# Strided slice: loads into 64 partitions with two rows each, one batch per queue, and joined stores

## Chip, cores, metric

One core of one Trainium2 chip. The metric is device time in microseconds (us) of one launch; a lower number is better. Each experiment was timed beside the kernel before on the same chip. A ratio is the mean time of one kernel's fast runs over that of the other's fast runs of the same rounds, so it is not quite the ratio of the medians that are quoted; a run that counts as slow is in the median and range, but not in the ratio. Faster or slower needs 2%; ratios are quoted with their 95% intervals.

## The reference

```python
# x is float32 [32, 1024, 512]; start, stop, stride = 0, 512, 2
def reference(x, start, stop, stride):
    return x[:, start:stop:stride, :].astype(np.float32)
```

The output is [32, 256, 512]: 256 rows of 2 KB out of each of 32 batches, every second row of the first half. 16.8 MB are read and 16.8 MB are written. Nothing is computed.

## The kernel before

Each batch has its 256 rows split by parity. Half of them go straight from HBM (the main memory) to HBM, issued by POOL. The other half go into SBUF (the memory on the core, 128 partitions), loaded by the queues of SP and ACT, and out again by SP's queue. SP, ACT and POOL are the units of the core that issue the transfers; one set of 16 DMA engines carries out those of all three queues (their shares of its time add up to 95.1%). `apart` chooses the parity, which alternates from one pair of batches to the next.

```python
def apart(b):
    return 1 - (b >> 1 & 1)

def two(t, b, step, parity):
    return t[b : b + step + 1 : step].rearrange("b (p two) d -> two p b d", two=2)[parity]

def tile_strided_slice_kernel(tc, x, start, stop, stride, out):
    ...                                                   # src = x[:, 0:512:2, :], P = 128, D = 512
        held = [io.tile([P, 2, D], x.dtype, name=f"held{i}") for i in range(B // 2)]
        for g in range(0, B, EIGHT):
            for i, (b, step) in enumerate(((0, 5), (2, 5), (1, 3), (3, 3))):
                b += g
                at = g + 2 * i
                (sp, act)[i % 2].dma_start(held[at // 2], two(src, at, 1, 1 - apart(at)))
                pool.dma_start(two(out, b, step, apart(b)), two(src, b, step, apart(b)))
        for b in range(B):
            to = out[b].rearrange("(p two) d -> two p d", two=2)[1 - apart(b)]
            sp.dma_start(to, held[b // 2][:, b % 2])
```

A load fills 128 partitions with one row of each of two batches (512 KB, "128x2" below). A store writes one batch (256 KB). There are 16 loads, 16 copies and 32 stores.

## Time and profile before

| | before |
|---|---|
| median (range), us | 80.34 (80.07 to 80.65), 4 runs |
| profiled execution, us; its span | 79.17; 77.4 |
| DMA queues | q1 = SP (loads, then stores), q10 = ACT (loads), q0 = POOL (copies) |
| first packet of SP, ACT, POOL, us | 1.83, 2.53, 6.21 |
| last packet of ACT's loads, of POOL's copies, us | 49.1, 55.7 |

The last packets are read from the packet records of the trace. The profiled execution of before is a little faster than its timed runs, so the two profiles lie 3.6 us apart where the medians lie 2.6 apart. The prediction's 80.57 us is the median of three runs.

### The profile page before, as it was taken

How to read it: one execution, taken by the hardware profiler on the slowest of the kernel's cores; microseconds unless marked ns; L12 is line 12 of the kernel's file. 1: busy time of each engine (PE TensorE's matmuls, PEld its weight loads, DVE VectorE, ACT ScalarE, POOL GpSimd, SP SyncE). 2: the span in 40 equal slices, each digit the busy share in tenths (PEclk: the TensorE clock that was granted, in tenths of full speed). 3: DMA queues.
4: the chain of work that ended last, by engine and by line, in shares of the span. 5: the costliest groups of instructions: out<-in, count | busy, mean ns of one | idle time of the engine just before them, and what ended most of it. 6: DMA issues, size and time to landing. Idle time of an engine off the chain costs nothing. (4 is left out here: it accounts for less than half of the span.)

```text
span 77.4 us, 113 instructions
## 1 busy us (share of the span) xinstructions
POOL 11.3 (15%) x20
## 2 busy tenths in 40 slices
POOL 4995003303023031130000000000000000000000
DMA  0799999999999999999999999999999999999960
GB/s 7 235 303 334 332 281 347 327 310 386 351 349 363 364 314 358 358 321 333 323 300 310 347 307 357 413 392 339 402 404 405 375 356 347 361 356 353 350 216 20
DMA packets 11264, 25.17 MB, mean 325 GB/s; under 512 B 1024, under 2 KB 1024, under 8 KB 11264
## 3 DMA queue, kind: packets, MB, share of 16 engines
q1 hardware_dynamic: 6784, 12.59, 48.1%
q0 software_dynamic: 2304, 8.39, 29.3%
q10 hardware_dynamic: 2176, 4.19, 17.7%
HBM read 16.78 MB, written 16.78 MB: 434 GB/s over the span
## 5 line engine op out<-in xcount | busy, mean ns | idle before, releaser
L37 POOL DMA_DIRECT2D out_dram<-in_x_dram x16 | 11.1, 696 | 22.6 <-DMA out_dram<-in_x_dram 21.8
L57 POOL MEMSET const-float32-0.0<- 128x1 f32 x1 | 0.1, 99 | 0.2 <-issue 0.2
L57 POOL MEMSET const-bfloat16-1.0<- 128x1 bf16 x1 | 0.1, 102 | 0.0
L57 POOL MEMSET const-uint8-127<- 128x1 uint8 x1 | 0.1, 100 | 0.0
L57 POOL MEMSET const-float32-1.0<- 128x1 f32 x1 | 0.1, 99 | 0.0
## 6 DMA issues: line engine op xcount, KB each, us to landing
out_dram<-in_x_dram POOLq DMA_DIRECT2D x16, 512.0 KB, 23.6
out_dram<-held SPq DMA_DIRECT2D x32, 256.0 KB, 6.1
held<-in_x_dram ACTq DMA_DIRECT2D x8, 512.0 KB, 22.9
held<-in_x_dram SPq DMA_DIRECT2D x8, 512.0 KB, 22.7
```

Of the source, the lines that this page charges most:

```text
L37: pool.dma_start(two(out, b, step, apart(b)), two(src, b, step, apart(b)))
L57: nc = _bacc.Bacc("TRN2", target_bir_lowering=False, num_devices=1)
```

## The change

The intent: one store of 512 KB for two neighbouring batches, half as many stores and waits. For this a partition must hold two rows of one batch, so the even batch of a pair goes to partitions 0 to 63 by SP's queue, the odd one to 64 to 127 by ACT's. Loads are now 32 of 256 KB ("64x2" below). The order of issue is fixed as written.

```diff
+def pairs(t, parity):
+    return t.rearrange("(p n two) d -> two p n d", n=2, two=2)[parity]
 ...
-    with tc.tile_pool(name="io", bufs=1) as io:
+    with tc.tile_pool(name="io", bufs=1) as io, tc.manual_schedule():
 ...
-                at = g + 2 * i
-                (sp, act)[i % 2].dma_start(held[at // 2], two(src, at, 1, 1 - apart(at)))
+                for k, queue in enumerate((sp, act)):
+                    at = g + 2 * i + k
+                    to = held[at // 2][P // 2 * k : P // 2 * (k + 1)]
+                    queue.dma_start(to, pairs(src[at], 1 - apart(at)))
                 pool.dma_start(two(out, b, step, apart(b)), two(src, b, step, apart(b)))
-        for b in range(B):
-            to = out[b].rearrange("(p two) d -> two p d", two=2)[1 - apart(b)]
-            sp.dma_start(to, held[b // 2][:, b % 2])
+        for b in range(0, B, 2):
+            to = out[b : b + 2].rearrange("b r d -> (b r) d")
+            sp.dma_start(pairs(to, 1 - apart(b)), held[b // 2])
```

## The prediction

> **What bounds the kernel now.** I read the page's busy slices first, then its queues, then the windows, then SyncE's waits. The kernel computes nothing: half of the rows go from HBM to HBM by POOL's queue, the other half into SBUF by the queues of SP and ACT, and out again by SP's. The slices and the queues of the page:
>
> ```profile
> DMA  0799999999999999999999999999999999999960
> GB/s 7 235 303 334 332 281 347 327 310 386 351 349 363 364 314 358 358 321 333 323 300 310 347 307 357 413 392 339 402 404 405 375 356 347 361 356 353 350 216 20
> DMA packets 11264, 25.17 MB, mean 325 GB/s; under 512 B 1024, under 2 KB 1024, under 8 KB 11264
> q1 hardware_dynamic: 6784, 12.59, 48.1%
> q0 software_dynamic: 2304, 8.39, 29.3%
> q10 hardware_dynamic: 2176, 4.19, 17.7%
> ```
>
> The 16 DMA engines are busy (9) from the third slice to the third from last, and the three queues' shares add to 95.1%. So the time is the packets' time: it can only fall if a packet gets cheaper, or fewer bytes move. 25.17 MB is 8.39 MB each of direct copies, loads and stores. Take 16 completion packets per transfer off: ACT's q10 has 8 transfers, so 2176 - 128 = 2048 packets for 4.19 MB, 2 KB each; POOL's q0 has 16, so 2304 - 256 = 2048 packets for 8.39 MB, 4 KB each. A mean packet took 0.177 x 16 x 77.4 us / 2048 = 107 ns on q10, and likewise 97 ns on SP's q1 (6144 packets of 2 KB), 177 ns on q0.
>
> The windows over the stages (us, POOL busy, clock, DMA share, GB/s):
>
> ```profile
> 1.80:6.20 4.40, 4.40 (x8) 1.00 0.87 270
> 6.20:49.00 42.80, 6.16 (x9) 1.00 1.00 336
> 49.00:56.00 7.00, 0.00 (x0) 1.00 1.02 383
> 56.00:60.00 4.00, 0.00 (x0) 1.00 1.06 407
> 60.00:72.00 12.00, 0.00 (x0) 1.00 1.06 357
> 72.00:77.40 5.40, 0.00 (x0) 1.00 0.53 184
> ```
>
> With loads in flight, engines that are just as busy move 336 GB/s; when only stores are left they reach 407, then 357. At 407 a 2 KB packet costs 16 x 2048 / 407 = 80 ns, so the 97 to 107 ns above hold a good deal of waiting inside packets. Measured against 407, the stretch 6.2 to 49 loses 42.8 x (1 - 336/407) = 7.5 us, 60 to 72 loses 1.5, and the end 72 to 77.4 loses 5.4 - 0.99/0.407 = 3.0, mostly engines that finish at different times, and the closing. That is all there is to win.
>
> SyncE's waits (total us, times, longest) and the issues:
>
> ```profile
> SPq L40 <- DMA held<-in_x_dram: 22.0, 4, 6.5
> SPq L36 <- DMA held<-in_x_dram: 19.8, 4, 5.7
> SPq L40 <- DMA out_dram<-held: 12.9, 24, 2.2
> out_dram<-in_x_dram POOLq DMA_DIRECT2D x16, 512.0 KB, 23.6
> out_dram<-held SPq DMA_DIRECT2D x32, 256.0 KB, 6.1
> held<-in_x_dram ACTq DMA_DIRECT2D x8, 512.0 KB, 22.9
> held<-in_x_dram SPq DMA_DIRECT2D x8, 512.0 KB, 22.7
> ```
>
> These are the issuer's waits, not the engines': loads wait for the load four before on their queue, and 24 of 32 stores for the store eight before. So eight hardware transfers are in flight at most. While the DMA share is 1.0 these waits cost nothing.
>
> [...] bytes in flight over landing time give POOL 8 x 0.524 MB / 23.6 us = 178 GB/s, ACT 4 x 0.524 / 22.9 = 92, SP 92: two to one to one[...]. [...] The loads of before step 2 MiB between their two batches; that this is why they lag is my guess, and only 336 against 407 GB/s supports it.
>
> **The change part by part.**
> *Loads.* 16 of 512 KB become 32 of 256 KB. An issue takes 0.40 us (median) on SP's or ACT's sequencer; 8 more each is 3.2 us over 40 us, beside the transfers: 0. Loads in flight fall from 8 x 0.524 = 4.2 to 2.1 MB. The first 2.1 MB last 2.1 / 0.270 = 7.8 us, and each slot refills as it lands, so the queues do not run dry: 0. By the same sum, a load should take 4 x 0.262 MB / 92 GB/s = 11.4 us to land instead of 22.8.
> *Packet size.* In before, the SBUF side of a load was already 4 KB in one piece per partition, and its packets were 2 KB, as the DRAM side was. Now it is again 4 KB against 2 KB, so I keep 2 KB packets and 11,264 of them: 0.
> *Order of reads.* A load no longer alternates between two batches 2 MiB apart; it takes rows 8 KB apart in one batch. If that takes some 13 of the 71 GB/s that the load stage lacks, it runs at 349: 14.4 MB / 0.349 = 41.2 us instead of 42.8, **-1.6**. Against that, SP and ACT now read neighbouring batches at the same time, of the same row parity.
> [...] **+1.0**. [...]
> *Stores.* 32 of 256 KB become 16 of 512 KB, so 16 fewer issues of 0.33 us, and 8 stores instead of 24 wait for an older one. With the engines never idle this frees nothing: 0. Bytes in flight double to 4.2 MB, and a store should take 4.2 MB / 0.36 = 11.7 us to land instead of 6.1. What can count is that a packet's neighbour is now the next row of the same parity and that one store covers two batches: of the 1.5 us lost in 60 to 72 and the like around it I give **-0.6**.
> *Fixed order* of issue: each queue was already in the order of the program: 0. POOL's direct copies: unchanged, 0.
> Sum: -1.6 + 1.0 - 0.6 = -1.2 us on 80.57, so **79.4 us**.
>
> **The rivals.** [...]
> *B, the load stage heals.* Read waits go away and the stage nears 380 GB/s: 14.4 / 0.38 = 37.9, -5 us, 75.5. For it: 383 GB/s in 49 to 56, where direct copies still read. Against: those copies, untouched, read as much as the loads do.
> *C, 4 KB packets.* If the hardware queues joined two rows in a packet, they could cost what q0's do, 177 instead of 194 ns per 4 KB: 512 x 17 ns x 0.5 = 4.4 us an engine, 76. Against: the loads of before did not.
> *D, nothing.* The engines' time per byte stays as it is, and 80.5 comes out.
>
> **Range and chances.** D and the central sum lie within 2% or at its edge (78.96); B and C and a good case of the order of reads lie below; A lies above 82.18. A tuned kernel is rarely restructured like this without an aim that reaches the memory, so I lean to the faster side: faster 0.42, same 0.39, slower 0.19. Eight times in ten: 76.3 to 82.4 us.
>
> **What the profile after would show.** Packets stay at 11,264 (C: fewer). Loads land in about 11.4 us and stores in 11.7. The load stage moves 349 GB/s (A: under 325; B: over 370), and q10's share falls slightly from 17.7% (A: over 20%). The stores-only stretch moves 360 to 375. DMA stays at 9 in the slices; a hole there would mean that half as many load bytes in flight starve a queue, which I excluded. The prediction fails if time per packet depends on something that I do not see[...].

The +1.0 us in the sum is the estimate for loads into one half of the partitions; before has no such loads, so its trace could not show the effect. Rival A is the same effect in full: loads into halves bind, by estimate 84 us.

## More of the kernel before

The view to read this kernel by is a table of stages: how many bytes all DMA engines moved in a stretch. Columns: stretch in us, its length, POOL's busy time (instructions), clock, mean busy share of the 16 DMA engines, GB/s. Kernel before:

```profile
0.00:8.00 8.00, 5.78 (x12) 1.00 0.71 226
8.00:16.00 8.00, 1.38 (x2) 1.00 0.99 321
16.00:48.00 32.00, 4.13 (x6) 1.00 1.00 337
48.00:56.00 8.00, 0.00 (x0) 1.00 1.02 387
56.00:72.00 16.00, 0.00 (x0) 1.00 1.06 369
```

The engines are busy from 8 us on, yet what they move changes with the mixture. Loads and copies together, which both read HBM, move 321 to 337 GB/s. From 48 us on, when the loads are done and stores run beside the last copies, it is 387.

## The result

The changed kernel takes 82.97 us (82.74 to 83.52, 4 runs) against 80.34: ratio 1.0336, 95% interval 1.0263 to 1.0409. It is **slower by 3.4%**; 79.4 us had been predicted, and the measured time lies outside the range.

From the page of the changed kernel, busy slices, rates and queues (packets, MB, share of 16 engines), then the issues (count, KB each, us to landing):

```profile
DMA  0799999999999999999999999999999999999830
GB/s 0 165 306 248 354 330 241 343 356 267 348 362 329 336 290 304 385 328 346 371 292 339 320 348 320 261 392 402 407 410 378 349 349 355 355 352 351 309 123 9
...
q1 hardware_dynamic: 6656, 12.58, 44.7%
q0 software_dynamic: 2304, 8.39, 30.6%
q10 hardware_dynamic: 2304, 4.20, 18.7%
...
out_dram<-in_x_dram POOLq DMA_DIRECT2D x16, 512.0 KB, 24.9
out_dram<-held SPq DMA_DIRECT2D x16, 512.0 KB, 11.8
held<-in_x_dram SPq DMA_DIRECT2D x16, 256.0 KB, 13.4
held<-in_x_dram ACTq DMA_DIRECT2D x16, 256.0 KB, 13.3
```

There is no hole in the busy slices and there are as many packets as before. What fell is the rate: the second and fourth slices show 165 and 248 GB/s where before showed 235 and 334, and the fast slices at the end of the loads begin one slice later (413 in the 26th before, 392 in the 27th after; a slice is 1.94 us before and 2.03 after). The stage table of the changed kernel:

```profile
0.00:8.00 8.00, 5.80 (x12) 1.00 0.68 177
8.00:16.00 8.00, 1.38 (x2) 1.00 0.99 316
16.00:48.00 32.00, 4.14 (x6) 1.00 1.01 333
48.00:56.00 8.00, 0.00 (x0) 1.00 0.99 338
56.00:72.00 16.00, 0.00 (x0) 1.00 1.06 372
```

Subtract it from the table of before, rate times length. The first 8 us lack 49 x 8 = 0.39 MB; 8 to 16 lacks 0.04; the 32 us from 16 to 48 lack only 0.13; 48 to 56 lacks 49 x 8 = 0.39; 56 to 72 gains 0.05. Together 0.90 MB, which at the 0.36 MB per us of the store stage is 2.5 us. So the loss sits **in two places, the first 8 us and the stretch 48 to 56**, and hardly in the long middle, where I had looked for the gain. The remaining 1.1 us of the two spans are at the end: in the changed kernel the engines finish over some 3.6 us, in before over 2.4.

In the second place before has stores and copies, whereas the changed kernel is still loading: ACT's queue moves 0.38 MB in this stretch instead of 0.04, and its last load packet comes at 55.6 us instead of 49.1. How that begins shows in the queues' packets (packets, MB, share) within the first 6.2 us. Kernel before:

```profile
q1 hardware_dynamic: 332, 0.65, 35.6%
q10 hardware_dynamic: 274, 0.54, 25.8%
```

Changed kernel, same stretch:

```profile
q10 hardware_dynamic: 192, 0.36, 27.9%
q0 software_dynamic: 90, 0.36, 20.3%
q1 hardware_dynamic: 144, 0.26, 12.2%
```

Before, the loads have the first 6.2 us to themselves and move 1.19 MB. In the changed kernel they move 0.62 MB, and POOL's copies have already moved 0.36 beside them. SP's first packet comes at 3.29 us instead of 1.83, POOL's at 3.94 instead of 6.21, though both issue their first transfers at the same times in the two traces (0.7 and 1.3 us). ACT's first packet is not late (2.18 us instead of 2.53): the two load queues have changed places, and the later of them starts 0.76 us later than before. The issue of a load also takes longer: a median of 0.53 us for 256 KB instead of 0.40 for 512 KB on SP.

### The profile page after: what moved, and what is told of

Its sections match the earlier page's. It is cut to its first block, busy times and chain, and to the rows that moved or that the text cites.

```text
span 81.0 us, 116 instructions
## 1 busy us (share of the span) xinstructions
POOL 11.3 (14%) x20
## 2 busy tenths in 40 slices
DMA packets 11264, 25.17 MB, mean 311 GB/s; under 512 B 1024, under 2 KB 1024, under 8 KB 11264
## 3 DMA queue, kind: packets, MB, share of 16 engines
q10 hardware_dynamic: 2304, 4.20, 18.7%
## 6 DMA issues: line engine op xcount, KB each, us to landing
out_dram<-held SPq DMA_DIRECT2D x16, 512.0 KB, 11.8
held<-in_x_dram SPq DMA_DIRECT2D x16, 256.0 KB, 13.4
held<-in_x_dram ACTq DMA_DIRECT2D x16, 256.0 KB, 13.3
```

## The experiments

Eighteen runs, all with the right result except those marked.

### Which part of the change: neighbours, queues, size or the halves

Three theories are set against each other: the halves theory (loads into one half of the partitions are slower, as in rival A), the neighbour theory (both queues read neighbouring batches at once) and the small-load theory (loads of half the size). Five runs tell them apart, one of them a repeat.

**ACT takes the pairs in another order**, so both queues never load neighbouring batches or one parity together.

```diff
-                    at = g + 2 * i + k
+                    at = g + 2 * (i ^ k) + k
```

The halves theory expected no change: 83.0 us, a ratio of 1.03, a load stage of 326 GB/s.

> The changed kernel, but ACT takes the pairs of a group in the order 1, 0, 3, 2, so SP and ACT never load the two batches of one pair, nor rows of one parity, at the same time. [...] Neighbour theory (both queues read neighbouring batches of one parity at once and collide in HBM): back to 80.4 us, ratio 1.00, load stage 336. Small-load theory (32 loads with half the bytes in flight): 83.0.

Measured: 81.86 us, ratio 1.0294 (1.0218 to 1.0370). The loss stays.

**Both halves of a pair on one queue**, pairs alternating.

```diff
-                    queue.dma_start(to, pairs(src[at], 1 - apart(at)))
+                    (sp, act)[i % 2].dma_start(to, pairs(src[at], 1 - apart(at)))
```

The halves theory expected 83 us or worse, up to 85.

> The changed kernel, but both halves of a pair are loaded by one queue, and the pairs alternate between SP and ACT as in the kernel before. [...] Neighbour theory: 80.4 us. Small-load theory: 83.0.

Measured: 82.23 us, 1.0332 (1.0275 to 1.0389). Together with the first run, the neighbour theory is out.

**One batch per load, but into 128 partitions** ("128x1"), on the kernel before.

```diff
-                (sp, act)[i % 2].dma_start(held[at // 2], two(src, at, 1, 1 - apart(at)))
+                for k, queue in enumerate((sp, act)):
+                    one = src[at + k].rearrange("(p two) d -> two p d", two=2)
+                    queue.dma_start(held[at // 2][:, k], one[1 - apart(at)])
```

The halves theory expected 80.4 us and a load stage of 336 GB/s.

> The kernel before (128 partitions, one row of a batch each, its own stores), but a load takes one batch, 256 KB, even batches on SP and odd ones on ACT. [...] Neighbour theory: 83 us, load stage 326. Small-load theory: 83 us, loads landing in about 13 us.

Measured: fast runs 1.0049 (0.9978 to 1.0119), but the four runs were 81.39, 81.38, 80.05 and 79.77, and the first two, the profiled one among them, count as slow. So I repeated it with five rounds:

> The kernel with one batch per load into 128 partitions once more, for its distribution. If halving the loads costs nothing: nearly all runs within 0.5% of before. If it makes an unsteady start: again some runs near 81.4 us, and the mean of all 1.01 to 1.015 times that of before.

Measured: 80.67 us (80.27 to 81.09), 1.0062 (1.0011 to 1.0112). Halving the loads costs about 0.6% by itself and is not the main cause. The 81.4 us did not come again.

**Two rows into every second partition** instead of one half, with stores batch by batch.

```diff
-                    to = held[at // 2][P // 2 * k : P // 2 * (k + 1)]
+                    to = held[at // 2][k::2]
 ...
+        for b in range(B):
+            sp.dma_start(pairs(out[b], 1 - apart(b)), held[b // 2][b % 2 :: 2])
```

The halves theory expected 80.4 us, and a share of ACT's queue under 18%.

> The changed kernel's loads (64 partitions, two rows each, even and odd batches on different queues), but into every second partition instead of one half, and stores batch by batch, 32 of 256 KB, as the layout asks. [...] Neighbour theory and small-load theory: 83 us.

Measured: 81.97 us, 1.0302 (1.0253 to 1.0350). So loading into one half of the partitions is not what costs the 3% in the full kernel. Left over are the 64-partition, two-row form itself and what it does to the other queues.

### Where in time: the first group, the stores, the order of rows

**First of four groups loaded and stored as before**, the other three as changed: the first group's loads are `two(src, at, 1, 1 - apart(at))` into `held[at // 2]`, alternating queues, with their old stores.

> The changed kernel, but the first of the four groups of eight batches is loaded and stored as in the kernel before (four loads of 512 KB into 128 partitions). The traces show the changed kernel 1.2 us behind by the time that 1.5 MB have moved, SP's first packet at 3.3 us instead of 1.8. Start-up theory (64-partition loads are slow to be turned into packets, which delays the start): the ratio to before falls from 1.033 to about 1.015, and 1.5 MB are there at 7.2 us. Steady theory (each load costs more, all through the load stage): a quarter of the loss goes, ratio 1.025.

Measured: 79.55 us, **1.0022** (0.9962 to 1.0081). Nearly the whole loss is gone, more than either theory had foreseen, although 24 of 32 loads are still 64x2 and 12 stores are still joined. Stage lines:

```profile
0.00:8.00 8.00, 5.77 (x12) 1.00 0.74 223
...
48.00:56.00 8.00, 0.00 (x0) 1.00 1.03 389
```

Both places are mended: 223 for 177, and 389 for 338. The second one is some 40 us after the only loads that were altered.

**The reverse**: before, with the first group as changed.

> The reverse: the kernel before, but the first group of eight batches is loaded into 64 partitions and stored as in the changed kernel. Start-up theory: ratio to before about 1.015. Steady theory: about 1.008. If the engines drift apart because of an early delay alone, up to 1.03.

Measured: 80.38 us, 1.0132 (1.0096 to 1.0167), what the start-up theory named. SP's first packet is at 3.2 us, POOL's at 4.0, and 1.5 MB are there at 8.1 us instead of 7.2. But it is 1.3% of the 3.4%: a changed first group alone does not bring the whole loss back.

**Stores joined, nothing else.**

```diff
-        for b in range(B):
-            to = out[b].rearrange("(p two) d -> two p d", two=2)[1 - apart(b)]
-            sp.dma_start(to, held[b // 2][:, b % 2])
+        for b in range(0, B, 2):
+            sp.dma_start(two(out, b, 1, 1 - apart(b)), held[b // 2])
```

> The kernel before with its own loads; only the stores are joined, two batches in one of 512 KB. Prediction's working: the store part is worth -0.6 us, ratio 0.993. Drift theory (512 KB stores let the 16 engines drift further apart, so that the last ends later): about 1.01, with the last 0.2 MB taking over 2 us.

Measured: 79.26 us, 0.9982 (0.9944 to 1.0020). The purpose of the change, half as many stores, is worth nothing that can be told from noise.

**Rows of a partition 512 KB apart** instead of 8 KB, on the run with every second partition: `"(n p two) d -> two p n d"` in `pairs`.

> The run with every second partition (ratio 1.030), but the two rows of a partition are 512 KB apart in x instead of 8 KB, in loads and stores. If the order in which an engine reads neighbouring rows costs the time (steady theory, HBM side): ratio falls to about 1.00 to 1.01. If the shape of the transfer (64 partitions by two) costs it: stays at 1.03.

Measured: 81.39 us, 1.0260 (1.0225 to 1.0295), against 1.0302. The difference of 0.4% lies within the two intervals (and the two runs were on different chips), so the order of rows does not explain the 3%, and nothing shows that neighbouring rows are the better ones.

### The loads by themselves

POOL's copies are taken out, so half of the output is missing and the results are wrong. Each was run once, so its state is unknown.

> The changed kernel without the direct copies, so half of the output is missing on purpose: it measures the 64-partition loads by themselves. Start-up theory: SP's first packet again at 3.2 us against ACT's 2.2, so about 1.05 us of making packets for each 256 KB load, one after the other for both queues; if that is the rate, loads alone run at no more than 0.262 / 1.05 = 250 GB/s, below the 300 to 330 of the kernel before in its first microseconds. If the late start has another cause (POOL's copies), SP starts by 2 us and the loads run at 320 or more.

> The same for the loads of one batch into 128 partitions, one row each, 256 KB too (half of the output missing on purpose). Start-up theory: both queues start by 2.0 us, and the loads alone run at 320 GB/s or more. The load stage's first 2 MB are there some 2 us sooner than with 64 partitions.

If one half of the partitions is what holds the loads at 237 GB/s, 300 GB/s or more was expected of the next run.

> Loads alone (half of the output missing on purpose), 64 partitions by two rows, but every second partition[...]. [...] If the shape (64 partitions, two rows) is: 237 again. SP's first packet at 3.2 us either way.

> The loads of the kernel before alone, 512 KB into 128 partitions (half of the output missing on purpose): 300 to 330 GB/s, first packets at 1.8 and 2.4 us. Were it near 237 too, the limit would have nothing to do with the 64 partitions.

Two stretches of the stage table (columns as above; GB/s last), 64x2 into halves:

```profile
0.00:4.00 4.00, 0.20 (x4) 1.00 0.38 98
...
8.00:24.00 16.00, 0.00 (x0) 1.00 1.07 241
```

64x2 into every second partition:

```profile
0.00:4.00 4.00, 0.20 (x4) 1.00 0.32 99
...
8.00:24.00 16.00, 0.00 (x0) 1.00 0.98 303
```

128x2, the loads of before:

```profile
0.00:4.00 4.00, 0.20 (x4) 1.00 0.50 121
...
8.00:24.00 16.00, 0.00 (x0) 1.00 1.02 330
```

128x1 had 154 and 314, a little under the 320 expected. Two separate effects appear. Alone, loads into halves are held to 241 GB/s, their packets near 147 ns (median; 84 in the other two), and putting the same loads into every second partition lifts them to 303: the halves do bind, *when loads have the engines to themselves*. The 303 also exceeds the 250 of the first expectation, so a rate of making packets of 1.05 us for each load is not the limit. Beside the copies the loads move only some 150 to 180 GB/s (in 16 to 48 us the queues of SP and ACT together move 173 in before and 166 in the changed kernel), which fits that every second partition brought nothing in the full kernel. The other effect is the start: in the first 4 us both 64x2 forms move 98 to 99, whatever their partitions; SP's first packet comes at 3.2 us in both.

If one half of the partitions holds the loads, about 237 GB/s again was expected here.

> Loads alone into half of the partitions, but one row per partition and load: 64 loads of 128 KB (half of the output missing on purpose). [...] If the two-row shape does: 280 or more, unless the issue of so small loads (0.33 us each, two queues, eight in flight) holds them.

One row per load into halves gave 232 GB/s in 8 to 24 us at a DMA share of 0.87, with half of the packets at 84 ns. The engines had gaps, so something else held its 128 KB loads as well, by estimate their number in flight. It does not tell the half from the shape: inconclusive.

### How little of the first group matters

**First group 128x1** (the loads of the third run; its stores one by one), the rest as changed.

> The changed kernel, but the first group of eight batches is loaded by the same number of loads of the same size on the same queues, into 128 partitions with one row each. If the shape of the first loads is the cause: ratio to before 1.00 to 1.005, as with the first group done as before. If the size of the first loads (512 KB, so more bytes in flight) was what helped there: 1.03.

Measured: 80.79 us, 1.0195 (1.0141 to 1.0249). A miss for both expectations: neither 1.00 nor 1.03. The loads start promptly (0.5 MB at 3.8 us), but lose it again when POOL starts, with 1.5 MB at 8.2 us. Yet this is not where its time goes: its stretch 48 to 56 moves 391 GB/s, and by 72 us its trace lacks only 0.10 MB against before, 0.3 us. The rest of the 1.6 us between the two spans lies at the very end, where the last packet comes at 77.5 us instead of 76.1. Why the engines finish so far apart, no run shows.

**Only the first load of each queue as before** (and the stores of these four batches).

> The changed kernel, but only the very first load of each queue is one of before (512 KB into 128 partitions); all others are as changed. If the first microseconds alone count: ratio 1.00 to 1.01, 1.5 MB there by 7.4 us. If it is the whole first group: about 1.02.

Measured: 80.74 us (79.80 to 81.59), 1.0137 (1.0057 to 1.0218). One of the four runs (81.59) counts as slow. The result lies between the two expectations: two of the 512 KB loads return over half of the loss by the mean, four return nearly all of it. Its profile is its fastest run (79.80), with 392 GB/s in 48 to 56, so it does not show where the others lose.

### The head start itself

In every full trace so far that begins with 64x2 loads, POOL's copies begin by 4.9 us (in most by 4.1) and ACT's loads end between 51.7 and 55.6 us. If what counts is that the loads get ahead of the copies, then holding POOL back must help the changed kernel, although it takes work away from engines that have room (a busy share of 0.68 in the first 8 us).

```diff
+        pool.memset(io.tile([P, 3072], x.dtype, name="late"), 0.0)
         for g in range(0, B, EIGHT):
```

> The changed kernel, but POOL fills an unused tile for some 2 us before its first copy, so its copies start near 6 us as in the kernel before (3.9 in the changed one). Head-start theory (the loads must get ahead of POOL's copies, or the stage in which both read lasts longer): ratio to before falls from 1.033 to 1.01 or 1.02, ACT's loads end by 53 us instead of 55.6. If POOL's early start is only a sign of something else in the start: 1.033 or more, as POOL loses 2 us in which engines have room.

Measured: 80.94 us, **1.0163** (1.0120 to 1.0207): half of the loss is gone by doing 2.66 us of useless work. POOL's first packet now comes at 9.5 us, later than I had aimed at, and ACT's loads end at 50.1. One of the six runs (81.75) counts as slow. Stage lines:

```profile
0.00:8.00 8.00, 7.47 (x12) 1.00 0.72 165
8.00:16.00 8.00, 1.60 (x3) 1.00 1.04 343
16.00:48.00 32.00, 4.82 (x7) 1.00 1.00 333
48.00:56.00 8.00, 0.00 (x0) 1.00 1.03 401
```

The first place stays bad (165). The loads start no faster, and from 4 to 8 us, without copies beside them, they move 238 GB/s, as they do alone (235): here the halves do hold them. The second place, 48 to 56, goes from 338 to 401. The middle is 333 as in the changed kernel. So the head start is what decides the second place.

The run with all loads 128x1 (five rounds) parts the head start from the total. Its first 8 us move 1.47 MB, hardly more than the changed kernel's 1.41 (before: 1.81). But 1.33 MB of them are loads and 0.15 copies; the changed kernel has 0.86 and 0.55, before 1.57 and 0.24. Its queues in the first 8 us, and its stretch 48 to 56:

```profile
q1 hardware_dynamic: 400, 0.75, 38.5%
q10 hardware_dynamic: 313, 0.58, 20.0%
q0 software_dynamic: 37, 0.15, 12.3%
...
48.00:56.00 8.00, 0.00 (x0) 1.00 1.03 388
```

The second place is whole, and the run loses 0.6%. So which bytes go first counts for more than how many have moved by 8 us. ACT's last load packet alone is a poor mark: it comes at 53.9 us here too, and its queue still moves 0.27 MB in 48 to 56 (0.38 in the changed kernel), yet the stretch moves 388 GB/s.

> The kernel before with the same delay of POOL, its copies starting near 8 us instead of 6.2. Head-start theory: no slower, perhaps 0.5 to 1% faster (ACT's loads end by 47 us instead of 49.1). Otherwise: 0 to 2 us slower, 1.00 to 1.02.

Measured: 79.53 us, 1.0007 (0.9974 to 1.0040). This lies in both expectations, so it decides nothing between them; the kernel before seems to have head start enough. Its stretch 48 to 56 moves 354 GB/s instead of 387 without any loss of time, while 16 to 48 moves 342 instead of 337 and 56 to 72 372 instead of 369: one stretch must be read with its neighbours. No run here beats the kernel before clear of noise.

## Why the prediction was wrong, step by step

- **"Loads ... do not run dry: 0."** This is the step that failed. I asked whether the queues would run dry, which they did not (DMA stays at 9 in the slices), and took for granted that they fill as fast as before: the 7.8 us for the first 2.1 MB are worked out with the old loads' 270 GB/s. They do not: 0.39 MB, 1.1 us at 0.36 MB per us, is missing by 8 us, and the loads' late start lets the copies share the engines from 3.9 us. The loads then end 6.5 us later, which costs another 0.39 MB in 48 to 56. That the start and the head start decide is shown by the first group as before (1.0022) and by POOL held back (1.0163). The reverse (1.0132) shows a limit: a changed first group alone costs 1.3% of the 3.4%, and the rest comes only with later loads that are changed too; why is not shown. The prediction's list of losses left the start out as well: its own window from 1.8 to 6.2 us moves 270 GB/s, which against 407 loses 4.4 x (1 - 270/407) = 1.5 us, but "all there is to win" is counted from 6.2 us on.
- **"Order of reads ... -1.6."** Failed: the middle stage moved 333 GB/s, not 349. With 512 KB between rows instead of 8 KB the ratio fell by 0.4%, within the two intervals. The 2 MiB between the batches of a load did not hold the old kernel back: its loads alone reach 330 GB/s, the most of all forms.
- **The +1.0 for loads into halves.** Real but not there: 241 against 303 GB/s alone, with packets near 147 ns against 84, but nothing clear of noise in the full kernel (1.0302 against the changed kernel's 1.0336). Alone, transfers of 128 partitions were faster than those of two halves (330 against 241). Rival A named 84 us and 83.0 came, but not by its mechanism. Its mark, a load stage under 325 GB/s, came close (326 in 6.2 to 49 us), yet it is an average over a slow start and a hardly changed middle.
- **"Stores ... -0.6."** Too large: 0.9982, about -0.14 us, within noise. That the waits free nothing was right. Their landing time of 11.7 us came out as 11.8.
- **"Packet size ... 0" and "Fixed order ... 0".** 11,264 packets as foreseen. Fixed order had no run of its own, but the run with the first group as before has it too and loses nothing that can be told from noise.
- **Loads landing in 11.4 us** came as 13.3 to 13.4; in 6.2 to 49 us all queues together moved 326 GB/s instead of 336. q10's share rose from 17.7% to 18.7% instead of falling.

What stays open: why loads of 64 partitions by two rows take longer to get going (SP's first packet came 2.6 us after its issue began, 0.73 to 3.29, instead of 1.1, 0.74 to 1.83); why POOL's packets come at 3.9 to 4.9 us beside such loads and at 5.3 to 6.7 beside the others, with the same time of issue; why a first group of 128x1 loads helps only half, when all loads of that form cost 0.6%; and the 1.1 us at the end of the profile, which no run isolates. Part of the 3.6 us between the two profiles is luck, as the profiled execution of before was faster (79.17 us) than all its timed runs; in which stage is not known.

## What to carry to other kernels

When the DMA engines are busy throughout, do not stop at the average: compare the bytes moved stage by stage and queue by queue, for a loss can sit in the first microseconds and show its second half 40 us later through the order in which queues finish (here 0.39 MB less by 8 us, and 0.39 MB less again in 48 to 56). Before changing the form of a transfer, look at how soon its first packets come and which other queue will take the engines in the meantime; here it paid that the loads, for which the stores wait, got ahead of the copies. Fewer and larger stores gained nothing here (0.9982), where only the issuer had been waiting.
